# Token sums made by accumulating transfers instead of VectorE operations, in a hybrid convolution and attention layer

## The chip, the cores and the metric

The kernel runs on one core of one Trainium2 chip. The metric is the time of one execution in device microseconds (us); a kernel's time is the median of several executions. Engines are written as the profile has them: PE is TensorE's matmul, PEld its weight load, DVE is VectorE, ACT is ScalarE, POOL is GpSimd and SP is SyncE. PSUM is the memory that matmuls write, SBUF the memory on the chip, DRAM the one outside.

## The reference, cut to what matters

One layer of a model with two groups of tokens, 128 context tokens and 512 sample tokens, 1024 channels each. All 640 tokens go through one input projection `w_in` of 10240 columns; a long convolution (by a Fourier transform) and a neighbourhood attention work on parts of it, and the results are gated, projected and merged.

```python
def layer_forward(x, cond, ctx_kv, p):
    shift, scale, gate = modulation(cond, p["w_ada"], p["b_ada"])
    h = x * (1 + scale) + shift
    (v_h, x1, x0, g_h), (q, k, v, g_a), m = split_projection(h, p["w_in"], p["conv_w"], p["conv_b"])
    h_fwd, h_bwd = hyena_filters(...)
    y_h = hyena_long_conv(v_h, x1, x0, h_fwd, h_bwd, p["hyena_d"])
    ...
    out = merge_branches(y_h, g_h, y_a.reshape(g_a.shape), g_a, m, p["w_bh"], p["w_ba"], p["w_out"])
    x_new = layer_norm(ALPHA * x + gate * out, p["ln_g"], p["ln_b"])

def split_projection(h, w_in, conv_w, conv_b):
    z = h @ w_in
    ...

def hyena_long_conv(v_h, x1, x0, h_fwd, h_bwd, d_bias):
    u = v_h * x1
    ...
    y = jnp.fft.irfft(uf * ff[None], n=n, axis=1)[:, :L].astype(u.dtype)
    return (y + u * d_bias) * x0
```

The token sums of this case are no part of that formula. They come from a way of multiplying 2 by 2 blocks of `h` and `w_in` with seven products instead of eight, in which four of the left factors are sums and differences of blocks of `h`.

## The kernel before, in words

Every f32 operand of a matmul is kept as two halves, a high one of type F32R and a low one with the rest: `h` is `hH + hL` (tiles of 128 channels by 640 tokens, eight of them in each), a weight tile is `wh + wl`, and a product is three matmuls, hH by wh, hL by wh and hH by wl (`mm3`, L182). `split` (L99 to 102) makes such a pair: ScalarE copies the high half (L101) and VectorE subtracts it from the source (L102). For some weights (`eng="dma"`, L161 to 163) the low half is made without VectorE: ScalarE writes minus the high half into wl, GpSimd issues a transfer that adds the weights from DRAM to it (L162), and ScalarE copies the high half.

The run has these stages. A prologue makes `h` (to about 46 us). Three quarters follow, to about 300 us: `quarter_head`, `quarter_tail` and `values` make projection tiles of the convolution branch and the attention's values; woven into them are `long_conv`, `long_conv_back` and `filter_spectrum`, the Fourier transforms of the signal and the filter. Each projection tile ends in `conv_tile`: ScalarE copies two PSUM banks into one of two buffers `zs` (L481 to 485), scales it into the tile (L487), and VectorE adds the two neighbours (L489, two operations). A bank is free for the next tile but one when ScalarE has copied it, and `zs` when the second L489 has read it. The `fl` matmuls (L400, L401) start a class of the filter spectrum: VectorE makes `sd` of them (L406), ScalarE and VectorE split it into `sh` and `sl`, and TensorE takes those for `fa`, `fb`, `fc`, `fd` (L170 to 172). `yb` is the transform back, and L637 adds its result to u. After the quarters (about 300 us) come attention and the pair products with the seven-product scheme, whose matmuls are `sp<-t,wb` (L1235).

In that scheme the blocks of `h` are (i, j): i one of two halves of the channel tiles, j one of two halves of the tokens (`CS[j]`); r picks two of the channel tiles. For r = 0 and 1, `token_sums(r)` makes four sums, t1 = h00 - h01, t3 = h11 - h01, t2 = t1 + h11 and t4 = t2 - h10, each from high and low halves, in the tiles ts00, ts01 (for r = 0) and ts10, ts11. Before, VectorE made them: L714, L717, L718, L722, L723 and L703 (`step`), 128 by 640 each. `keep` splits each sum into high and low (the tiles t1.. to t4.., L101 and L102) and stores both in `tok_d` in DRAM by two transfers on GpSimd's queue (L712). Later `load_sums` reads them back; the first of these loads goes out at 304.7 us.

The order of the work comes from generators: `along` advances the token sums by one step after every sixth step of the quarter's main generator, and `weave` mixes main and convolution. Within the quarters a scheduler then chooses the order on each engine by its own estimates; only instructions marked with `keep_in_program_order` stay as written. Transfers of GpSimd are issued in the order of its queue, and a transfer that has to wait holds those behind it. The weight tiles are in rings: `raw` and `wh` two buffers, `wl` three.

Of the kernel before, what the change touches and what calls it, by code (L numbers as in the profile page):

```python
# [10 lines left out]
F32R = mybir.dt.float32r  # L11
AF = mybir.ActivationFunctionType
# [33 lines left out]
def tile_hyena_natten_step(ctx: ExitStack, tc: tile.TileContext, a, o):  # L46
    nc = tc.nc
    P = 128

    def f(ap):  # L50
        return ap.bitcast(F32)
# [4 lines left out]
    def two(t):  # L56
        return t.rearrange("p (a b) -> p a b", a=2)
# [10 lines left out]
    def weave(main, side, n_main, n_side):  # L68
        done, taken = 0, 0
        for _ in main:  # L70
            done += 1
            while taken * n_main < done * n_side:
                if next(side, StopIteration) is StopIteration:
                    break
                taken += 1
        for _ in side:
            pass
# [22 lines left out]
    def split(dst_h, dst_l, src, eng=None):  # L100
        hi = nc.scalar.activation(dst_h, src, AF.Copy)  # L101
        return hi, (eng or nc.vector).tensor_tensor(dst_l, src, f(dst_h), op=ALU.subtract)  # L102


    def row(pool, tag, name, dt=F32, bufs=NK + 1, n=NT):
        return pool.tile([P, NT + 4 if tag == "yh" else NT], dt, tag=tag, bufs=bufs, name=name)[:, :n]
# [395 lines left out]
    def quarter_head(q):  # L502
        us = []
        out[f"u{q}"] = us
        for i in range(2):
            n = 2 * q + i
            u = hw.tile([P, NG + 1], F32, tag="u", bufs=4, name=f"u{n}")
            x1 = hwa.tile([P, NG + 1], F32, tag="cv", bufs=2, name=f"x1_{n}")
            yield from conv_tile(n, u)
            yield  # L510
            yield from conv_tile(8 + n, x1)
            nc.vector.tensor_tensor(u[:, :NG], u[:, :NG], x1[:, :NG], op=ALU.mult)
            us.append(u)
            yield
# [10 lines left out]
    def quarter_tail(q):  # L525
        for i in range(2):
            n = 2 * q + i
            out["x0"][n] = row(yhp, "yh", f"x0_{n}", n=NG + 1)
            yield from conv_tile(16 + n, out["x0"][n])
            gate_conv(n)  # L530
            yield
# [111 lines left out]
    def values(m, home=None):  # L643
        w = [wtile(T_V + 2 * m + i, "dma", width=256) for i in range(2)]
        ps = [acc(f"v{m}_{i}") for i in range(2)]

        def passes(k):
            wh, wl = w[k // 4][0][k % 4], w[k // 4][1][k % 4]
            return ((hH, wh, k == 0, False), (hL, wh, False, False), (hH, wl, False, k == NK - 1))

        for half in range(2):
            ks = range(4 * half, 4 * half + 4)
            for k in ks:
                for x, wk, first, last in passes(k):
                    for t in range(4):
                        nc.tensor.matmul(  # L656
                            ps[t // 2][:, t % 2 * 256 : t % 2 * 256 + 256], x[:, k, P * t : P * t + P], wk,
                            start=first and t % 2 == 0, stop=last, skip_group_check=True,
                        )
                yield  # L660
            if half:
                parts = [ps[0][:], ps[1][:]]
            else:
                pe = acc(f"ve{m}")
            for k in ks:
                for x, wk, first, last in passes(k):
                    nc.tensor.matmul(pe[:, :256], x[:, k, P * 4 :], wk, start=first, stop=last, skip_group_check=True)  # L667
            yield
        if home is None:
            v = out[f"v{m}"] = slot(m, "v", f"v{m}")  # L670
            for c, p in ((0, parts[0]), (512, parts[1]), (1024, pe[:, :256])):
                nc.scalar.activation(v[:, c : c + p.shape[-1]], p, AF.Copy)
        else:
            for i, p in enumerate(parts):
                v = hwa.tile([P, NG + 1], F32, tag="cv", bufs=2, name=f"v{m}_{i}")
                nc.scalar.activation(v[:, :512], p, AF.Copy)
                nc.scalar.activation(v[:, 512:640], pe[:, 128 * i : 128 * i + 128], AF.Copy)
                nc.sync.dma_start(home[m][:, 512 * i : 512 * i + 512], v[:, :512])
                nc.sync.dma_start(home[m][:, 1024 + 128 * i : 1152 + 128 * i], v[:, 512:640])
                if i == 0:  # L680
                    nc.sync.dma_start(o["new_v"][:, m * 256 : m * 256 + 256], v[:, :256])
            yield
            return
        nc.sync.dma_start(o["new_v"][:, m * 256 : m * 256 + 256], v[:, :256])
        yield
# [11 lines left out]
    def token_sums(r):  # L697
        def part(t, i, j):
            return f(t[:, 4 * i + 2 * r : 4 * i + 2 * r + 2, CS[j]])

        def step(dst, i, j, op):
            for t in (hH, hL):
                nc.vector.tensor_tensor(dst, dst, part(t, i, j), op=op)  # L703

        a_, b_ = (two(row(yhp, "yh", f"ts{r}{i}")) for i in range(2))

        def keep(name, t):
            at_ = 4 * SUMS.index(name) + 2 * r
            hi, lo = (row(yhp, "yh", f"{name}{r}{i}", F32R) for i in range(2))
            split(two(hi), two(lo), t)  # L710
            for i, x in enumerate((hi, lo)):
                nc.gpsimd.dma_start(tok_d[at_ + i], f(x))  # L712

        ins = nc.vector.tensor_tensor(a_, part(hH, 0, 1), part(hL, 0, 1), op=ALU.add)  # L714
        tc.keep_in_program_order(ins)
        yield
        nc.vector.tensor_tensor(b_, part(hH, 0, 0), a_, op=ALU.subtract)  # L717
        nc.vector.tensor_tensor(b_, b_, part(hL, 0, 0), op=ALU.add)  # L718
        yield
        keep("t1", b_)  # L720
        yield
        nc.vector.tensor_tensor(a_, part(hH, 1, 1), a_, op=ALU.subtract)  # L722
        nc.vector.tensor_tensor(a_, a_, part(hL, 1, 1), op=ALU.add)  # L723
        yield
        keep("t3", a_)
        yield
        step(b_, 1, 1, ALU.add)
        yield
        keep("t2", b_)
        yield  # L730
        step(b_, 1, 0, ALU.subtract)
        yield
        keep("t4", b_)
        yield

    def braid(x, y):
# [8 lines left out]
    def chain(*gens):  # L745
        for g in gens:
            yield from g
# [11 lines left out]
    def along(main, side, every):  # L759
        for i, _ in enumerate(main):  # L760
            if i % every == 0:
                next(side, None)
            yield

    for q in range(3):
        weave(along(chain(quarter_head(q + 1), quarter_tail(q), values((2, 3, 1)[q], v_d)), sums, 6),
              chain(long_conv(q), braid(long_conv_back(q), filter_spectrum(q + 1))), 6 * NK + N_VALUES, N_CONV + N_BACK + N_FILTER)
    ident = out["ident"]

# [934 lines left out]
```

## Time and profile before

| what | us |
|---|---|
| median of 3 runs | 890.14 |
| lowest and highest | 889.31, 892.96 |
| the profiled execution | 889.48 |
| its span (first to last instruction) | 887.7 |
| busy: TensorE, VectorE, ScalarE, GpSimd | 869.3, 637.0, 450.6, 190.6 |
| token sums on VectorE, first and last | 67.6, 196.2 |
| token sums' stores issued, first and last | 72.3, 197.3 |

The profile shows one execution. A row of the timeline has its start, its length, the engine, the line, the operation with what it writes and reads (`out<-in`), and in brackets how long the engine had been idle and what ended that. A row of a group has its count behind an x, the busy time and the mean. A row of waits has the engine and line that waited, whom for, the total, the number and the longest. A row of transfers has the queue (SPq, POOLq), the count, the size of one and the median time from issue to landing.

### The profile page before, as it was taken

To read this page: it belongs to the slowest core of one execution; us is meant where nothing else is said; L and a number is where in the kernel's file an instruction comes from. 1 tells how busy PE (TensorE), PEld (TensorE's weight loads), DVE (VectorE), ACT (ScalarE), POOL (GpSimd) and SP (SyncE) were. 2 spreads that over 40 slices of the span, in tenths; PEclk is the share of its full clock that TensorE was granted. 3 is DMA by queue.
4 is the path that set the end of the run, shared out by engine and by line. 5 is a ranking of instruction groups with operands and counts; after the bars stand their busy time and mean duration, and the time that the engine had idled before them with its cause. 6 is when DMAs were issued, how large, how long until landed. Compare 5 with 4: busy or idle time off the path is not lost.

```text
span 887.7 us, 17134 instructions
## 1 busy us (share of the span) xinstructions
PE 869.3 (98%) x6476; PEld 837.6 (94%) x6476; DVE 637.0 (72%) x1215; ACT 450.6 (51%) x956; POOL 190.6 (21%) x216
## 2 busy tenths in 40 slices
PE   8999999899999999999999999999999999999996
PEld 6899999899899999899999999999999999999885
DVE  4779592996688459488877777777877666766666
ACT  4396454754554544467656566666566632243200
POOL 0012010221101021129354334333554200000000
PEclk9999999999999999999999999999999999999999
DMA  8978576678546697798686758675854576545521
GB/s 323 399 168 232 117 176 128 179 208 188 135 99 161 149 221 153 230 339 262 158 252 149 226 146 245 155 198 168 235 125 127 193 283 239 174 162 188 186 86 56
DMA packets 75247, 169.09 MB, mean 190 GB/s; under 512 B 11004, under 2 KB 28668, under 8 KB 75165
## 3 DMA queue, kind: packets, MB, share of 16 engines
q1 hardware_dynamic: 56204, 123.06, 41.4%
q0 software_dynamic: 13632, 39.33, 23.3%
q10 hardware_dynamic: 5328, 5.61, 1.8%
q8 instruction: 51, 0.84, 0.4%
q14 instruction: 32, 0.25, 0.1%
HBM read 143.32 MB, written 23.99 MB: 188 GB/s over the span
## 4 chain that ended last, share of the span: by engine, by line
PE 93%; DVE 4%; ACT 1%; DMA 1%; issue 0%; POOL 0%; SPq 0%; POOLq 0%; DVEq 0%; ACTq 0%
PE mm L182 34%; PE sp L1235 29%; PE out L1514 6%; PE v L656 5%; PE s L1041 2%; PE s L948 2%; PE pt L1032 2%; PE ve L667 1%; PE adaT L252 1%; DMA t<-tok_d 1%; DVE x L489 1%; PE yb L171 1%; PE adaT L269 1%; PE yb L172 1%; PE yb L170 0%
## 5 line engine op out<-in xcount | busy, mean ns | idle before, releaser
L1235 PE MATMUL sp<-t,wb 128*128 128x320 f32 x1008 | 159.0, 311 | 0.2 <-DMA t<-tok_d 0.2
L1235 PEld LDWEIGHTS sp<-t,wb 128*128 128x128 f32 x1008 | 150.0, 188 | 1.0 <-issue 0.5
L1235 PE MATMUL sp<-hH,wb 128*128 128x320 f32 x500 | 121.1, 313 | 0.0
L182 PE MATMUL mm<-hH,wh 128*128 128x320 f32 x336 | 83.9, 315 | 5.4 <-ACT zs L484 4.2
L1235 PEld LDWEIGHTS sp<-hH,wb 128*128 128x128 f32 x500 | 86.1, 188 | 2.6 <-issue 2.6
L162 POOL DMA_DIRECT2D wl<-wall x34 | 30.5, 897 | 255.6 <-ACT wl L161 239.0
L182 PE MATMUL mm<-hH,wl 128*128 128x320 f32 x336 | 82.4, 311 | 0.4 <-DVE wl L102 0.4
L182 PE MATMUL mm<-hL,wh 128*128 128x320 f32 x336 | 81.9, 310 | 0.0
L1235 PE MATMUL sp<-hL,wb 128*128 128x320 f32 x250 | 77.2, 309 | 0.0
L182 PEld LDWEIGHTS mm<-hH,wh 128*128 128x128 f32 x336 | 57.4, 188 | 8.0 <-ACT zs L484 5.1
L163 ACT ACTIVATE wh<-raw 128x1024 fp32r<-128x1024 f32 x34 | 36.1, 1062 | 56.7 <-PE mm L182 41.5
L1196 DVE TENSOR_TENSOR wb<-s,wb 128x512 fp32r<-128x512 f32 x63 | 45.3, 721 | 18.9 <-ACT wb L1188 18.7
L182 PEld LDWEIGHTS mm<-hH,wl 128*128 128x128 f32 x336 | 57.5, 188 | 1.2 <-DVE wl L102 0.9
L182 PEld LDWEIGHTS mm<-hL,wh 128*128 128x128 f32 x336 | 57.3, 188 | 0.6 <-DVE hL L329 0.5
L1003 POOL TENSOR_SCALAR p<-p,sm 128x384 f32<-128x384 f32 x32 | 52.0, 1721 | 22.7 <-PE sp L1235 9.3
L1003 POOL TENSOR_SCALAR edge<-edge,sm 128x320 f32<-128x320 f32 x32 | 42.9, 1500 | 62.1 <-DVE sm L1001 62.1
L1188 ACT ACTIVATE wb<-s 128x512 fp32r<-128x512 f32 x63 | 39.7, 631 | 31.1 <-PE sp L1235 19.3
L1235 PEld LDWEIGHTS sp<-hL,wb 128*128 128x128 f32 x250 | 47.0, 188 | 0.0
L1514 PE MATMUL out<-woh,yhs 128*128 128x512 f32 (+1 forms) x176 | 45.7, 373 | 0.0
L1223 DVE TENSOR_TENSOR spare_hHp<-sp,yu 128x320 f32<-128x320 f32 x63 | 30.5, 484 | 17.7 <-PE sp L1235 10.7
L182 PE MATMUL mm<-yhs,wh 128*128 128x320 f32 x224 | 42.0, 309 | 0.0
L1514 PEld LDWEIGHTS out<-woh,yhs 128*128 128x128 f32 x176 | 32.0, 188 | 6.4
(415 smaller groups left out, 2253.3 us busy)
## 6 DMA issues: line engine op xcount, KB each, us to landing
raw<-wall SPq DMA_DIRECT2D x54, 512.0 KB, 3.8
wl<-wall POOLq DMA_DIRECT2D x34, 512.0 KB, 6.7
ra<-wall SPq DMA_DIRECT2D x21, 512.0 KB, 5.0
rb<-wall SPq DMA_DIRECT2D x40, 256.0 KB, 5.4
ada<-wada SPq DMA_DIRECT2D x16, 512.0 KB, 8.0
tm<-bias SPq DMA_DIRECT2D x16, 512.0 KB, 7.5
s<-wall SPq DMA_DIRECT2D x21, 256.0 KB, 5.2
s<-wall POOLq DMA_DIRECT2D x21, 256.0 KB, 4.6
```

The source lines that it names most:

```text
L162: nc.gpsimd.dma_start(wl, a["wall"][i], accum_op=ALU.add)
L163: nc.scalar.activation(wh, raw[:], AF.Copy)
L182: nc.tensor.matmul(ps[hf][:, :HALF], wt[k], x[:, hf * HALF : (hf + 1) * HALF], start=(i == 0 and k == 0), stop=(i == lead[2] and k == NK - ...
L656: nc.tensor.matmul(ps[t // 2][:, t % 2 * 256 : t % 2 * 256 + 256], x[:, k, P * t : P * t + P], wk, start=first and t % 2 == 0, stop=last, ...
L948: nc.tensor.matmul(dst[h], x[rows(h), qs], y[rows(h), ks], start=i == 0, stop=i == 2, skip_group_check=True)
L1003: nc.gpsimd.tensor_scalar_mul(pv, pv, sm[:, 2, c : c + 1])
L1032: nc.tensor.transpose(pt[:, i * P : i * P + P], ps[h][:, c : c + P], ident)
L1188: nc.scalar.activation(made[g][:, 0], block(g), AF.Copy)
L1196: nc.vector.tensor_tensor(made[g][:, 1], block(g), f(made[g][:, 0]), op=ALU.subtract)
L1223: nc.vector.tensor_tensor(c, dst, c if j == 3 else ps["u"], op=ALU.add)
L1235: nc.tensor.matmul(dst, wk, x(xi, k), start=j < 4 and k == 0 and i == 0, stop=k == 3 and i == 2, skip_group_check=True,)
L1514: ins = nc.tensor.matmul(dst, m[k][:, c0 : c0 + P], w[:, c : c + n], start=(first and k == 0), stop=(last and k == 5), skip_group_check=True,)
```

## The change

`token_sums` no longer uses VectorE. Each sum is formed in its tile by transfers on GpSimd's queue: a plain copy of a block of hH, then accumulating ones (`accum_op=ALU.add`) for hL and the further blocks. A difference needs a turned sign: ScalarE multiplies the tile by -1 in place (`turned`). For the halves, ScalarE writes minus the sum into the low tile and the high half into the high tile (`halves`), and a transfer adds the sum to the low tile (`rest`); then both are stored as before. For each r that is 3 copies, 13 accumulating transfers and the same 8 stores, and on ScalarE 2 turns and 4 times 2 activations where 4 copies were. All these transfers are marked to stay in program order. A group has 16 steps, where there were 9, and `along` advances them after every fifth step of main instead of every sixth.

```diff
@@ -698,39 +698,71 @@
         def part(t, i, j):
             return f(t[:, 4 * i + 2 * r : 4 * i + 2 * r + 2, CS[j]])
 
-        def step(dst, i, j, op):
-            for t in (hH, hL):
-                nc.vector.tensor_tensor(dst, dst, part(t, i, j), op=op)
-
-        a_, b_ = (two(row(yhp, "yh", f"ts{r}{i}")) for i in range(2))
-
-        def keep(name, t):
-            at_ = 4 * SUMS.index(name) + 2 * r
-            hi, lo = (row(yhp, "yh", f"{name}{r}{i}", F32R) for i in range(2))
-            split(two(hi), two(lo), t)
-            for i, x in enumerate((hi, lo)):
-                nc.gpsimd.dma_start(tok_d[at_ + i], f(x))
-
-        ins = nc.vector.tensor_tensor(a_, part(hH, 0, 1), part(hL, 0, 1), op=ALU.add)
-        tc.keep_in_program_order(ins)
-        yield
-        nc.vector.tensor_tensor(b_, part(hH, 0, 0), a_, op=ALU.subtract)
-        nc.vector.tensor_tensor(b_, b_, part(hL, 0, 0), op=ALU.add)
-        yield
-        keep("t1", b_)
-        yield
-        nc.vector.tensor_tensor(a_, part(hH, 1, 1), a_, op=ALU.subtract)
-        nc.vector.tensor_tensor(a_, a_, part(hL, 1, 1), op=ALU.add)
-        yield
-        keep("t3", a_)
-        yield
-        step(b_, 1, 1, ALU.add)
-        yield
-        keep("t2", b_)
-        yield
-        step(b_, 1, 0, ALU.subtract)
-        yield
-        keep("t4", b_)
+        def queued(dst, src, **how):
+            tc.keep_in_program_order(nc.gpsimd.dma_start(dst, src, **how))
+
+        def add(dst, src):
+            queued(two(dst), src, accum_op=ALU.add)
+
+        def turned(t):
+            nc.scalar.activation(t, t, AF.Copy, scale=-1.0)
+
+        a_, b_ = (row(yhp, "yh", f"ts{r}{i}") for i in range(2))
+        kept = {}
+
+        def halves(name, t):
+            hi, lo = kept[name] = [row(yhp, "yh", f"{name}{r}{i}", F32R) for i in range(2)]
+            nc.scalar.activation(lo, t, AF.Copy, scale=-1.0)
+            nc.scalar.activation(hi, t, AF.Copy)
+
+        def rest(name, t):
+            add(f(kept[name][1]), two(t))
+            store(name, 0)
+
+        def store(name, i):
+            queued(tok_d[4 * SUMS.index(name) + 2 * r + i], f(kept[name][i]))
+
+        queued(two(b_), part(hH, 0, 0))
+        queued(two(a_), part(hH, 0, 1))
+        yield
+        add(b_, part(hL, 0, 0))
+        add(a_, part(hL, 0, 1))
+        yield
+        turned(a_)
+        yield
+        add(b_, two(a_))
+        yield
+        halves("t1", b_)
+        add(a_, part(hH, 1, 1))
+        yield
+        rest("t1", b_)
+        add(a_, part(hL, 1, 1))
+        yield
+        store("t1", 1)
+        add(b_, part(hH, 1, 1))
+        yield
+        halves("t3", a_)
+        add(b_, part(hL, 1, 1))
+        yield
+        rest("t3", a_)
+        yield
+        store("t3", 1)
+        queued(two(a_), part(hH, 1, 0))
+        yield
+        halves("t2", b_)
+        add(a_, part(hL, 1, 0))
+        yield
+        rest("t2", b_)
+        turned(a_)
+        yield
+        store("t2", 1)
+        add(b_, two(a_))
+        yield
+        halves("t4", b_)
+        yield
+        rest("t4", b_)
+        yield
+        store("t4", 1)
         yield
 
     def braid(x, y):
@@ -763,7 +795,7 @@
             yield
 
     for q in range(3):
-        weave(along(chain(quarter_head(q + 1), quarter_tail(q), values((2, 3, 1)[q], v_d)), sums, 6),
+        weave(along(chain(quarter_head(q + 1), quarter_tail(q), values((2, 3, 1)[q], v_d)), sums, 5),
               chain(long_conv(q), braid(long_conv_back(q), filter_spectrum(q + 1))), 6 * NK + N_VALUES, N_CONV + N_BACK + N_FILTER)
     ident = out["ident"]
```

In the changed kernel the transfers have L702, the turn L708, the halves L715 and L716; lines below `token_sums` are 32 higher.

What GpSimd's queue holds at the first group, from the first weight tile of the quarters on. The names: `wl2`, `wl10`, `wl3`, `wl11` are low halves of weight tiles, `ts00` and `ts01` the sums under way, `t100` and `t101` the high and low half of t1. Before:

```order
L162 DMA wl2_894<-wall 128x1024
L162 DMA wl10_1046<-wall 128x1024
L162 DMA wl3_1127<-wall 128x1024
L162 DMA wl11_1235<-wall 128x1024
L712 DMA tok_d_81<-t100_1087 128x640
L712 DMA tok_d_81<-t101_1088 128x640
```

The changed kernel there:

```order
L162 DMA wl2_894<-wall 128x1024
L702 DMA ts01_907<-hH_85 128x2x320
L702 DMA ts00_906<-hH_85 128x2x320
L702 DMA ts01_907<-hL_87 128x2x320
L162 DMA wl10_1047<-wall 128x1024
L702 DMA ts00_906<-hL_87 128x2x320
L162 DMA wl3_1124<-wall 128x1024
L702 DMA ts01_907<-ts00_906 128x640
L162 DMA wl11_1235<-wall 128x1024
L702 DMA ts00_906<-hH_85 128x2x320
L702 DMA t101_1192<-ts01_907 128x640
L702 DMA tok_d_81<-t100_1191 128x640
```

Seven transfers of the sums have moved in between and behind the weight tiles, each accumulating one behind the transfer whose result it needs; the add of hL into ts00 stands behind wl10, and wl3 and wl11 stand behind adds.

ScalarE at the halves of t3 in the first group. `zs` is the copy of a PSUM bank, `x1_2` a convolution tile, `sh0_1`, `sh0_3` and `sh0_4` are high halves for the filter spectrum, `raw16`, `wh16` and `wl16` a weight tile, `t300` and `t301` the halves of t3, `t200` the high half of t2. Before:

```order
L161 ACTIVATE wl16_1332<-raw16_1329 128x1024
L101 ACTIVATE sh0_1_781<-sd0_1_779 128x512
L101 ACTIVATE t300_1247<-ts00_906 128x640
L487 ACTIVATE x1_2_890<-zs1_109,pack2_380 128x641
L101 ACTIVATE t200_1403<-ts01_907 128x640
L101 ACTIVATE sh0_3_818<-sd0_3_816 128x512
L163 ACTIVATE wh16_1331<-raw16_1329 128x1024
L481 ACTIVATE zs0_105<-mm3_0_1131 128x128
```

The changed kernel there:

```order
L485 ACTIVATE zs1_109<-mm10_1_1052 128x8x40
L161 ACTIVATE wl16_1329<-raw16_1326 128x1024
L715 ACTIVATE t301_1384<-ts00_906 128x640
L716 ACTIVATE t300_1383<-ts00_906 128x640
L487 ACTIVATE x1_2_890<-zs1_109,pack2_380 128x641
L101 ACTIVATE sh0_3_818<-sd0_3_816 128x512
L101 ACTIVATE sh0_4_853<-sd0_4_851 128x512
L163 ACTIVATE wh16_1328<-raw16_1326 128x1024
L481 ACTIVATE zs0_105<-mm3_0_1128 128x128
```

Two activations of t3 stand ahead of `x1_2` and `sh0_3`, and wait for the transfer that completes ts00; the copy of t2 has left this place.

VectorE between the two L489 of the tile `x0_1`, towards the end of the first quarter. `sd1_3` and `sl1_3` belong to the filter spectrum, `u0` and `u1` are the convolution's signal (L628, L637), `yu0` and `yu1` its product with the gate x0, `t401` is the low half of t4. Before:

```order
L102 TENSOR_TENSOR sl1_3_1526<-sd1_3_1523,sh1_3_1525 128x512
L489 SCALAR_TENSOR_TENSOR x0_1_1470<-zs1_109,pack2_380,x0_1_1470 128x641
L637 SCALAR_TENSOR_TENSOR u0_676<-u0_676,hyd0_713,y0_1546 128x4x128
L637 SCALAR_TENSOR_TENSOR u1_733<-u1_733,hyd0_713,y1_1634 128x4x128
L102 TENSOR_TENSOR t401_1617<-ts01_907,t400_1616 128x640
L489 SCALAR_TENSOR_TENSOR x0_1_1470<-zs1_109,pack2_380,x0_1_1470 128x641
```

The changed kernel there:

```order
L102 TENSOR_TENSOR sl1_3_1522<-sd1_3_1519,sh1_3_1521 128x512
L489 SCALAR_TENSOR_TENSOR x0_1_1466<-zs1_109,pack2_380,x0_1_1466 128x641 x2
L637 SCALAR_TENSOR_TENSOR u0_676<-u0_676,hyd0_713,y0_1544 128x4x128
L471 TENSOR_TENSOR yu1_1632<-x0_1_1466,u1_733 128x128
L637 SCALAR_TENSOR_TENSOR u1_733<-u1_733,hyd0_713,y1_1626 128x4x128
```

The two L489 have come together, the L637 pair stands behind them, and t401 is gone. On TensorE the `fl1_3` matmul, which `sd1_3` reads, stands 88 rows ahead of the next tile's first matmul (mm13), where it stood 39 rows ahead; in the second quarter `fl2_3` stands 83 rows ahead of mm15's, where it stood 38; and the first `fc` of `sh0_3` stands at row 566 of TensorE, where it stood at 583.

## The prediction

> **What bounds the kernel now.** I read the page first: the busy shares, then the chain that ended last.
>
> ```profile
> span 887.7 us, 17134 instructions
> PE 869.3 (98%) x6476; PEld 837.6 (94%) x6476; DVE 637.0 (72%) x1215; ACT 450.6 (51%) x956; POOL 190.6 (21%) x216
> PE 93%; DVE 4%; ACT 1%; DMA 1%; issue 0%; POOL 0%; SPq 0%; POOLq 0%; DVEq 0%; ACTq 0%
> ```
>
> TensorE is busy for 98% of the span, and 93% of the last chain is its own work. The change leaves its work alone, so all it can save is TensorE's idle time in the stretch in which the sums are made and used. Next I read the table of windows from 60 to 400 us (columns: window, its length, PE, PEld, DVE, ACT, POOL busy, PE clock, DMA share, GB/s). Besides the first two rows, these are the windows in which TensorE is not busy all the time; in the others it shows 20.00 of 20.
>
> ```profile
> 60.00:80.00 20.00, 20.00 (x138) 19.82 (x138) 18.41 (x25) 14.22 (x29) 4.30 (x7) 1.00 0.82 205
> 80.00:100.00 20.00, 20.00 (x145) 19.81 (x143) 15.37 (x25) 10.49 (x21) 3.00 (x5) 1.00 0.77 197
> 140.00:160.00 20.00, 18.86 (x136) 18.22 (x134) 8.18 (x14) 8.61 (x12) 2.31 (x4) 1.00 0.54 114
> 160.00:180.00 20.00, 18.13 (x125) 17.64 (x126) 20.00 (x34) 13.03 (x30) 4.42 (x8) 1.00 0.69 188
> 220.00:240.00 20.00, 18.19 (x130) 17.46 (x129) 9.29 (x16) 9.47 (x16) 2.14 (x3) 1.00 0.53 113
> 240.00:260.00 20.00, 19.36 (x141) 19.09 (x140) 15.62 (x28) 12.00 (x29) 1.62 (x3) 1.00 0.45 107
> 340.00:360.00 20.00, 19.36 (x131) 18.34 (x129) 15.04 (x23) 10.19 (x19) 1.72 (x2) 1.00 0.56 113
> 360.00:400.00 40.00, 38.95 (x272) 37.49 (x273) 27.47 (x69) 20.99 (x55) 8.32 (x13) 1.00 0.99 319
> ```
>
> The idle time is 1.14 + 1.87 + 1.81 + 0.64 + 0.64 + 1.05 = 7.15 us, the ceiling of any gain here. VectorE is full around 60 and 160 us, where token sums stand, yet TensorE waits for nothing around 60. What it does wait for is in the list of TensorE's waits, from 130 to 182 us and then from 182 to 300:
>
> ```profile
> PE mm L182 <- ACT zs L484: 2.5, 1, 2.5
> PE c_X L171 <- DVE ul L102: 0.5, 1, 0.5
> ...
> PE mm L182 <- ACT zs L484: 1.8, 1, 1.8
> PE ut L540 <- ACT F L451: 0.6, 1, 0.6
> ```
>
> Together 5.4 us. The timeline shows how the first arises, and the second has the same form, of which its last row shows the end:
>
> ```profile
> 153.83 0.69 DVE L406 TENSOR_TENSOR sd<-fl,dec 128x512 f32<-128x512 f32 x1 [6.80 <-PE fl L401]
> 156.10 0.89 DVE L489 SCALAR_TENSOR_TENSOR x<-zs,pack,x 128x641 f32<-128x641 f32 x1
> 156.90 2.20 DVE L637 SCALAR_TENSOR_TENSOR u<-u,hyd,y 128x512 f32<-128x512 f32 x2
> 159.03 0.80 DVE L102 TENSOR_TENSOR t<-ts,t 128x640 fp32r<-128x640 f32 x1
> 159.76 0.87 DVE L489 SCALAR_TENSOR_TENSOR x<-zs,pack,x 128x641 f32<-128x641 f32 x1
> 160.72 0.28 ACT L481 ACTIVATE zs<-mm 128x128 f32<-128x128 f32 x1 [2.13 <-DVE x L489]
> 238.10 0.28 ACT L481 ACTIVATE zs<-mm 128x128 f32<-128x128 f32 x1 [2.05 <-DVE x L489]
> ```
>
> TensorE waits for a PSUM bank that ScalarE copies into zs; ScalarE waits until VectorE's second L489 has read the old zs; VectorE came to that late, because it had idled 6.80 us for fl (placed late on TensorE) and because two L637 and one `t` of the sums stood between its two L489.
>
> **The change, VectorE's side.** Eighteen `ts` operations and eight `t` go:
>
> ```profile
> L101 ACT ACTIVATE t<-ts x8: 722/748/812, 71.3 to 192.3; 128x640 fp32r<-128x640 f32 x8
> L102 DVE TENSOR_TENSOR t<-ts,t x8: 804/816/824, 74.0 to 196.2; 128x640 fp32r<-128x640 f32 x8
> L714 DVE TENSOR_TENSOR ts<-hH,hL x1: 820/820/820, 67.6 to 67.6; 128x640 f32<-128x640 f32 x1
> ```
>
> These are the copies that ScalarE makes of the sums, the eight `t` of VectorE, and the first of the eighteen: 26 x 0.815 = 21.2 us of VectorE, nearly all beside TensorE's work. What they are worth is the waits above. In the changed order the two L489 before the first wait follow each other with no L637 or `t` between (the L637 pair and the `t` are 2.20 + 0.80 = 3.0 us, more than the 2.5 of the wait), and fl stands 88 rows of TensorE ahead of the waiting matmul instead of 39. At 20 us for 136 matmuls that is 49 x 0.147 = 7.2 us earlier. The 1.8 has the same form, with 83 rows instead of 38. I take both as gone, and with them the 0.5 and 0.6, which depend on the same late VectorE: **-5.4 us**. Between 0 (they come back elsewhere) and -7.15, this is the end that the rows explain.
>
> **The transfers.** On GpSimd's queue 32 transfers join the 16 stores: 26 accumulating ones and 6 copies, 327,680 bytes each. No row shows a 320 KB accumulate. The nearest, by issue to landing (the windows 60 to 80, 80 to 100 and 150 to 180, then the page, then the tile `t`):
>
> ```profile
> wl<-wall POOLq DMA_DIRECT2D x3, 512.0 KB, 7.1
> tok_d<-t POOLq DMA_DIRECT2D x4, 320.0 KB, 5.4
> ...
> tok_d<-t POOLq DMA_DIRECT2D x3, 320.0 KB, 6.6
> ...
> tok_d<-t POOLq DMA_DIRECT2D x6, 320.0 KB, 3.1
> ...
> raw<-wall SPq DMA_DIRECT2D x54, 512.0 KB, 3.8
> wl<-wall POOLq DMA_DIRECT2D x34, 512.0 KB, 6.7
> s<-wall SPq DMA_DIRECT2D x21, 256.0 KB, 5.2
> s<-wall POOLq DMA_DIRECT2D x21, 256.0 KB, 4.6
> q0 software_dynamic: 13632, 39.33, 23.3%
> ...
> DMA to landing us min/median/max: 2.5/5.1/6.8
> ```
>
> `wl` and the POOLq `s` accumulate already. The first sums stand where the DMA share is 0.82 and 0.77, so a link lands between 5.4 and 7.1 us; I take L = 6.0, midway between the two stores of the same size there. Wherever it is quiet, 3 to 4.6 is nearer.
>
> These links are in series, and ScalarE now waits inside its own order for three of them (turned, the t1 halves, the t3 halves). With these rows the first group can be laid out:
>
> ```profile
> 49.23 1.02 POOL L162 DMA_DIRECT2D wl<-wall  x1 [47.70 <-ACT wl L161]
> 56.59 0.87 POOL L162 DMA_DIRECT2D wl<-wall  x1 [6.34 <-ACT wl L161]
> 62.51 0.93 ACT L487 ACTIVATE x<-zs,pack 128x641 f32<-128x641 f32 x1
> 81.69 0.63 ACT L101 ACTIVATE sh<-sd 128x512 fp32r<-128x512 f32 x1 [2.35 <-DVE sd L406]
> 85.95 0.27 PE L170 MATMUL fc<-sh,dftH 128*128 128x256 f32 x1
> ```
>
> The first copies go out behind the `wl` of 49.23; the add of hL into ts00 stands behind the `wl` of 56.59, so it goes at 57.5 and lands at 57.5 + L. ScalarE turns it (0.75, as a `t<-ts`; ScalarE comes there at 62.5). Three links follow, each waiting for the last: ts01 += ts00, ts00 += hH, ts00 += hL. The t3 halves can start at 57.5 + L + 0.85 + 3L = 58.35 + 4L: 78.4 for L = 5, 82.4 for 6, 86.8 for 7.1. Behind them on ScalarE stand the L487 of x1 and `sh` for TensorE's `fc`. The `fc` of 85.95 stands 17 rows earlier in the changed order, 17 x 0.145 (20 us for 138 matmuls) = 2.5 us, so `sh` must end by 83.4. Less 0.63 for itself, 0.93 for L487 and 2 x 0.75 for the halves, the sum must have landed by 80.3. Cost = 58.35 + 4L - 80.3: 0 up to L = 5.5, **2.1 us at 6.0**, 4.4 at 6.6, 6.4 at 7.1. The `wl` that now queue behind blocked links are covered by three buffers; the one at 56.59 keeps its place.
>
> The other groups (from about 130 us on) run where windows show shares of 0.45 to 0.69 and most links land before ScalarE comes: 0 to 2, I take **0.5**. ScalarE's own extra (8 lows and 4 turns, 12 x 0.75 = 9 us) lies in an engine busy 8.6 to 14.2 of 20: nothing. The 10.5 MB added need, at queue q0's rate (39.33 MB in 23.3% of 887.7 us, 190 GB/s), 55 us of all 16 engines. That is why L is not taken at its quiet value.
>
> Against this change speaks a rule of the Trainium skill: "Collectives: The Full Stack", section on the bandwidth ceiling, says that an adding transfer needs two source reads and moves at about half the rate of a copy. The pair raw 3.8 and wl 6.7 agrees, the pair `s` 5.2 and 4.6 does not. By it a link would be nearer 5.4 x 1.76 = 9.5 us (an estimate), and the first group alone would cost 16: the stretched case below, driven further.
>
> **Sum.** The profiled execution took 889.48 (887.7 and 1.8 outside): 889.48 - 5.4 + 2.1 + 0.5 = 886.7. The median shown, 890.14, lies 0.66 above, so the forecast is 887.3. About 0.5% (4.45 us) is what a measurement of this kernel can tell from no change: faster means below 885.7, slower above 894.6.
>
> **Rivals.** *All hidden.* Links land in 5.5 us or less even at the start, the groups cost nothing: 884.1, by the median 884.7, with the ceiling 882.9. For: lone stores land in 2.5 to 3.1. Against: 5.4 and 6.6 in the very windows. In the Trainium skill, "DMA: Bandwidth & Descriptors", the section on one SWDGE transfer fits 2.0 us plus bytes over 436 GB/s, 2.75 us here (an estimate), which leads to this case; only the minimum of 2.5 in the trace agrees, the median of 5.1 does not.
>
> *The links stretch.* The copies, adds and stores of the first group saturate a queue already at 0.8, and a link takes 8 us. `wl` in that window shows 7.1 without this load. The t3 halves then wait until 90.35, `sh` and TensorE with them: 10 us, and 1 elsewhere: 889.48 - 5.4 + 10 + 1 = 895.1, by the median 895.8. It decides above L = 7.8; up to 6.6 it is repaid.
>
> *The waits come back.* The scheduler has moved matmuls earlier everywhere, and the new place meets its producers as late as the old one: the gain is 0 to 2 and the cost stays, 890 to 893. For: VectorE is at 20.00 of 20 in the window 160 to 180, which shows how little freedom its neighbours have. Against: the wait's cause (the L637 pair and `t` between two L489) is gone from the order.
>
> **Chances.** Forecast (L from 5.5 to 6.6, the waits gone; 885 to 889.6) 0.40, all hidden 0.24, waits back 0.18, stretched 0.18. Faster: all hidden and 0.06 of the forecast's lower end, 0.30. Slower: stretched and 0.04 of waits back with some stretch, 0.22. Same: the rest, 0.48. For 8 in 10 the range takes the hidden case down to its ceiling, 883, and the stretched one up to L = 8.2 (11 + 1), 897.
>
> **What would show it.** In the changed profile: no `mm <- ACT zs` wait near 160 and 237 us (if they are there, the gain's step is wrong); ts and t transfers on POOLq landing in 5.5 to 6.6 us at 50 to 90 us (this decides between hidden, forecast and stretched); ScalarE waiting for `ts` by about 2 us at each of three places before 90, TensorE for `fc <- sh` by 2. A wait of TensorE for `wl`, or for W's halves at `yb`, would be a cost that I set at nothing.

## The result and the profile after

The changed kernel takes 916.33 us (median of 4 runs, 914.93 to 918.93), the kernel before 890.88 beside it (4 runs): ratio 1.029, interval 1.025 to 1.032. The change makes the kernel slower by some 25 us, where 887.3 was forecast.

The page of the profile after, its span, the busy shares and the chain that ended last:

```profile
span 912.9 us, 17166 instructions
...
PE 879.2 (96%) x6476; PEld 846.8 (93%) x6476; DVE 620.0 (68%) x1189; ACT 459.1 (50%) x968; POOL 221.9 (24%) x248
...
PE 75%; issue 10%; DMA 8%; DVE 3%; ACT 2%; POOL 2%; POOLq 0%; ACTq 0%; DVEq 0%
```

Two things are seen. TensorE's own part of the chain has fallen from 93% to 75%; transfers now hold 8% of it and "issue" 10%. These shares are not a loss by themselves: 48.2 us of "issue" are GpSimd's idle time from 1.5 to 49.7 us, which stands in the chain because the chain now leads back through its queue. And TensorE's busy time has grown, 869.3 to 879.2, with the same 6476 matmuls. So the 25.2 us of span are 9.9 us of slower matmuls and 15.3 us more idle (33.7 for 18.4).

The table of windows, those of 20 us (the last of 40) between 60 and 400 us in which TensorE idles (columns as in the prediction):

```profile
60.00:80.00 20.00, 16.94 (x103) 16.13 (x102) 9.95 (x14) 10.79 (x24) 8.11 (x9) 0.91 0.92 179
80.00:100.00 20.00, 17.54 (x113) 16.93 (x112) 11.31 (x20) 10.86 (x22) 7.50 (x8) 0.91 1.04 227
...
180.00:200.00 20.00, 17.84 (x122) 17.00 (x121) 11.19 (x18) 11.02 (x23) 7.14 (x8) 1.00 1.02 243
200.00:220.00 20.00, 16.79 (x135) 16.52 (x134) 17.07 (x22) 11.40 (x20) 6.54 (x7) 0.97 0.91 202
...
260.00:280.00 20.00, 16.15 (x114) 15.62 (x112) 5.66 (x9) 9.72 (x19) 5.95 (x8) 1.00 0.97 218
280.00:300.00 20.00, 18.63 (x129) 18.36 (x130) 15.93 (x18) 8.34 (x15) 3.68 (x5) 0.83 0.62 152
...
360.00:400.00 40.00, 35.37 (x226) 34.01 (x226) 27.32 (x43) 15.07 (x27) 5.03 (x10) 0.91 0.62 168
```

The idle time is 20.7 us, where it was 7.1, in three places at which sums are made (5.5 us from 60 to 100, 5.4 from 180 to 220, 5.2 from 260 to 300) and behind the last quarter (4.6 from 360 on). The clock column falls to 0.91 and 0.83 in windows with gaps. The DMA share in the first window rose from 0.82 to 0.92, in the second from 0.77 to 1.04.

The waits of TensorE over the whole run, those above 1 us in 60 to 400:

```profile
PE c_X L170 <- ACT uh L101: 3.8, 2, 2.1
PE mm L182 <- DMA wl<-wall: 3.7, 2, 3.2
PE p_X L170 <- ACT uh L101: 3.2, 1, 3.2
PE fb L170 <- ACT sh L101: 2.6, 1, 2.6
PE yb L170 <- ACT ph L101: 2.5, 1, 2.5
PE fc L170 <- ACT sh L101: 2.5, 1, 2.5
PE yb L171 <- DVE pl L102: 1.2, 1, 1.2
```

The four waits that the prediction took away (`mm <- ACT zs` twice, `c_X <- DVE ul`, `ut <- ACT F`) are gone. In their place TensorE waits for operands that ScalarE makes (`sh`, `uh`, `ph`) and for `wl`. Why ScalarE is late is in its own waits (40 to 320 us) for the turns L708 and the halves L715:

```profile
ACT t L715 <- DMA ts<-ts: 13.5, 3, 5.1
...
ACT t L715 <- DMA ts<-hL: 10.9, 2, 6.2
ACT ts L708 <- DMA ts<-hL: 7.6, 2, 7.3
...
ACT ts L708 <- DMA ts<-hLp: 4.1, 1, 4.1
```

That is 36.1 us in eight waits, where before it waited for no transfer of the sums. The first group in the timeline, GpSimd's issues, ScalarE's two long waits and TensorE's answer to the second:

```profile
50.49 1.77 POOL L702 DMA_DIRECT2D ts<-hH  x2
59.40 1.21 POOL L702 DMA_DIRECT2D ts<-hL  x1 [7.13 <-DMA ts<-hH]
60.13 1.43 POOL L162 DMA_DIRECT2D wl<-wall  x1
60.74 2.05 POOL L702 DMA_DIRECT2D ts<-hL  x1
...
70.31 0.74 ACT L708 ACTIVATE ts<-ts 128x640 f32<-128x640 f32 x1 [7.32 <-DMA ts<-hL]
...
75.61 1.19 POOL L702 DMA_DIRECT2D ts<-hH  x1 [0.70 <-DMA ts<-ts]
...
83.86 1.20 POOL L702 DMA_DIRECT2D ts<-hL  x1 [5.56 <-issue]
89.00 0.74 ACT L715 ACTIVATE t<-ts 128x640 fp32r<-128x640 f32 x1 [6.22 <-DMA ts<-hL]
...
91.75 0.38 PE L170 MATMUL fc<-sh,dftH 128*128 128x256 f32 x1 [2.46 <-ACT sh L101]
```

The first add went out 8.9 us behind the copies that it needs (50.49 to 59.40; the copies land after 8.6), and the add that stands between two `wl` took 9.5 us (60.74 to 70.31). The t3 halves start at 89.0. And the transfers' times over the run:

```profile
tok_d<-t POOLq DMA_DIRECT2D x16, 320.0 KB, 5.6
...
ts<-hH POOLq DMA_DIRECT2D x8, 320.0 KB, 7.5
ts<-hL POOLq DMA_DIRECT2D x8, 320.0 KB, 6.3
t<-ts POOLq DMA_DIRECT2D x8, 320.0 KB, 6.6
...
ts<-ts POOLq DMA_DIRECT2D x4, 320.0 KB, 5.5
...
ts<-hHp POOLq DMA_DIRECT2D x2, 320.0 KB, 9.5
```

The rows of accumulating links have medians of 5.5 to 6.6 us. The plain copies are not below them: both of `ts<-hHp` (9.5) and four of the eight `ts<-hH` are copies, the other four are adds.

The slower matmuls are seen in windows of 4 us at the gaps (columns as above; the clock is the third from the end):

```profile
88.00:92.00 4.00, 1.54 (x11) 1.27 (x10) 0.79 (x1) 2.69 (x4) 0.18 (x1) 1.00 1.13 234
92.00:96.00 4.00, 4.00 (x21) 3.82 (x21) 4.00 (x8) 2.67 (x7) 1.19 (x1) 0.59 0.95 172
...
280.00:284.00 4.00, 2.63 (x10) 2.44 (x11) 2.92 (x5) 1.35 (x4) 1.43 (x3) 0.55 0.77 180
284.00:288.00 4.00, 4.00 (x23) 4.00 (x23) 2.86 (x6) 3.69 (x8) 1.36 (x2) 0.59 0.63 209
```

After the gap of 2.46 us that ends at 91.75, TensorE does 21 matmuls in 4 us where it does 29 to 32 at full clock in the windows around. At the gap of 3.17 that ends at 281.37 the lower clock lasts for some 7 us.

### The profile page after: what moved, and what is told of

The parts are those of the page before. It is cut to its first block, busy times and chain, and to the rows that moved or that the text cites. A ratio compares the mean times of both kernels' runs of the same rounds, so it can differ in the third digit from the quotient of the medians.

```text
span 912.9 us, 17166 instructions
## 1 busy us (share of the span) xinstructions
PE 879.2 (96%) x6476; PEld 846.8 (93%) x6476; DVE 620.0 (68%) x1189; ACT 459.1 (50%) x968; POOL 221.9 (24%) x248
## 4 chain that ended last, share of the span: by engine, by line
PE 75%; issue 10%; DMA 8%; DVE 3%; ACT 2%; POOL 2%; POOLq 0%; ACTq 0%; DVEq 0%
PE sp L1267 29%; PE mm L182 22%; PE out L1546 6%; PE v L656 4%; DMA ts<-hL 2%; PE s L1073 2%; PE s L980 2%; PE pt L1064 2%; DMA ts<-ts 1%; DMA ts<-hH 1%; DMA wl<-wall 1%; PE ve L667 1%; DMA ts<-hLp 1%; DMA t<-ts 1%; POOL ts L702 1%
## 5 line engine op out<-in xcount | busy, mean ns | idle before, releaser
L182 PE MATMUL mm<-hH,wh 128*128 128x320 f32 x336 | 81.4, 315 | 1.2 <-ACT hH L328 0.6
L162 POOL DMA_DIRECT2D wl<-wall x34 | 32.8, 969 | 196.6 <-ACT wl L161 164.6
L182 PEld LDWEIGHTS mm<-hH,wh 128*128 128x128 f32 x336 | 57.5, 191 | 2.7 <-ACT hH L328 0.8
L1035 POOL TENSOR_SCALAR p<-p,sm 128x384 f32<-128x384 f32 x32 | 50.1, 1646 | 23.7 <-PE sp L1267 9.8
L489 DVE SCALAR_TENSOR_TENSOR x<-zs,pack,x 128x641 f32<-128x641 f32 x32 | 28.3, 883 | 35.0 <-ACT x L487 34.4
```

The lines of the kernel that those rows point to most:

```text
L162: nc.gpsimd.dma_start(wl, a["wall"][i], accum_op=ALU.add)
L182: nc.tensor.matmul(ps[hf][:, :HALF], wt[k], x[:, hf * HALF : (hf + 1) * HALF], start=(i == 0 and k == 0), stop=(i == lead[2] and k == NK - ...
L489: nc.vector.scalar_tensor_tensor(d, zs[:, c : c + NG], convw[:, i, c : c + 1], d, op0=ALU.mult, op1=ALU.add)
L1035: nc.gpsimd.tensor_scalar_mul(pv, pv, sm[:, 2, c : c + 1])
```

## The experiments

The theories: A, ScalarE in its order waits for links of 6 to 9.5 us and holds TensorE's operands behind them; B, the added traffic and the longer GpSimd queue cost by themselves; C, the scheduler's new order costs by itself. All ratios are to the kernel before, timed beside the variant.

**One half alone: low halves by transfer** (lows_only), sums on VectorE:

```diff
-            split(two(hi), two(lo), t)
-            for i, x in enumerate((hi, lo)):
-                nc.gpsimd.dma_start(tok_d[at_ + i], f(x))
+            nc.scalar.activation(two(lo), t, AF.Copy, scale=-1.0)
+            nc.scalar.activation(two(hi), t, AF.Copy)
+            nc.gpsimd.dma_start(f(two(lo)), t, accum_op=ALU.add)
+            nc.gpsimd.dma_start(tok_d[at_], f(hi))
+            kept.append((tok_d[at_ + 1], f(lo)))
```

The last store goes out at the next step of the generator.

> Half of the change alone: the sums stay on VectorE, only their low halves are made by ScalarE (minus the sum, and the high half) and one accumulating transfer, with the store of the low half one step later. ScalarE waits for no transfer here. Theory A (links of 6 to 9.5 us, for which ScalarE waits in its order): 885 to 890, no gap of TensorE of 2 us or more that before did not have. Theory B (the added traffic and the blocked GpSimd queue cost by themselves): a quarter of the transfers, 893 to 897. Theory C (a new order by the scheduler costs by itself): cannot be told in advance, anything from 885 to 897, with the loss after the last values matmul.

893.73 us, ratio 1.001 (1.000 to 1.003): no change that can be measured. The time lies outside A's range and inside B's and C's, and TensorE has a new gap of over 2 us, which A did not allow. Two rows suggest why A's gain stayed out, one of TensorE's waits and one of VectorE's timeline:

```profile
PE fz L390 <- issue: 3.7, 1, 3.7
```

```profile
186.72 0.82 DVE L703 TENSOR_TENSOR ts<-ts,hH 128x640 f32<-128x640 f32 x1 [7.61 <-DMA t<-ts]
```

VectorE wants to form t2 over t1, which a transfer still reads, and stands for 7.61 us; TensorE's gap of 3.7 us, which the profile puts down to "issue", ends 3.0 us behind that start. That the one led to the other is tried in the last experiment (lows_own_tile).

**The other half alone: sums by transfers** (sums_only), low halves by `split` on VectorE:

```diff
-            nc.scalar.activation(lo, t, AF.Copy, scale=-1.0)
-            nc.scalar.activation(hi, t, AF.Copy)
+            split(hi, lo, t)
 
         def rest(name, t):
-            add(f(kept[name][1]), two(t))
             store(name, 0)
```

> The other half alone: the sums are made by transfers and ScalarE's turn as in the changed kernel, the low halves by VectorE as before. ScalarE still waits for the sums at the same six places per group. Theory A: 908 to 918, with ScalarE's waits for transfers near 60 to 70 and 82 to 89 us still there. Theory B: three quarters of the transfers, 907 to 912. Theory C: the loss after the last values matmul decides, 905 to 916.

907.7 us, ratio 1.018 (1.014 to 1.022): in B's and C's ranges and 0.3 us below A's, so it decides nothing between them. ScalarE still waits 30.4 us for transfers of the sums, as A has it. The run shows that most of the loss comes with the sums. TensorE's two longest waits in 60 to 400 us:

```profile
PE fc L170 <- ACT sh L101: 3.5, 1, 3.5
PE fa L170 <- ACT sh L101: 2.9, 1, 2.9
```

**ScalarE without the waits** (act_free), all transfers in place:

```diff
-            nc.scalar.activation(t, t, AF.Copy, scale=-1.0)
+            nc.scalar.activation(two(spare_), part(hH, 0, 1), AF.Copy, scale=-1.0)
...
-            nc.scalar.activation(lo, t, AF.Copy, scale=-1.0)
-            nc.scalar.activation(hi, t, AF.Copy)
+            nc.scalar.activation(two(lo), part(hH, 0, 1), AF.Copy, scale=-1.0)
+            nc.scalar.activation(two(hi), part(hH, 0, 1), AF.Copy)
```

> The changed kernel with all its 48 transfers in the same chain on GpSimd's queue, but ScalarE's turns and halves read a block of hH, which is ready, instead of the sums (so the sums are not computed rightly: signs and high halves are left out). ScalarE waits for no transfer of the sums. Theory A: 887 to 896, the gaps of TensorE for sh, uh and ph gone, at most 3 to 4 us left for a late wl. Theory B: 908 to 916, since traffic and queue are as in the changed kernel. Theory C: 896 to 902, the 6 us after the last values matmul stay.

894.77 us, ratio 1.004 (1.002 to 1.006): 21.6 us below the changed kernel, with the same 48 transfers in the same chain. This is in A's range and below both B's and C's. TensorE's busy time is 869.4 again, so the slower matmuls have gone together with ScalarE's waits. What stays are waits for `wl`, the list of TensorE's waits in 60 to 400:

```profile
PE mm L182 <- DMA wl<-wall: 4.6, 2, 3.4
PE v L656 <- DMA wl<-wall: 1.9, 4, 0.9
```

These 6.5 us are B's part.

**More room for each transfer** (paced), two empty steps of the generator ahead of each step of ScalarE (one ahead of the second turn), and a step after every third of main:

```diff
+        yield
+        yield
         turned(a_)
...
+        yield
+        yield
         yield
         halves("t1", b_)
...
-        weave(along(chain(...), sums, 5),
+        weave(along(chain(...), sums, 3),
```

> The changed kernel with the same work, but every step on ScalarE put two generator steps further behind its transfer (27 steps, one after every third step of main, instead of 16 after every fifth). Theory A: the transfers get about 13 us of main's work where they had 7, so ScalarE's waits fall under 1 us each and the time to 890 to 902. Theory B: as the changed kernel, 912 to 918. Theory C: 900 to 916 with gaps of TensorE that name no transfer.

914.87 us, ratio 1.025 (1.021 to 1.029): none of A's gain, a time in B's and C's ranges. But the room was not given: ScalarE's waits for the sums are 41.4 us, where A asked for under 1 us each. The timeline of ScalarE shows the turn and the t1 halves where they were in the changed kernel (70.31 and 75.40 there):

```profile
69.80 0.74 ACT L708 ACTIVATE ts<-ts 128x640 f32<-128x640 f32 x1 [6.74 <-DMA ts<-hL]
...
74.88 0.76 ACT L715 ACTIVATE t<-ts 128x640 fp32r<-128x640 f32 x1
```

The transfers are marked to stay in program order, ScalarE's steps are not; those go where the scheduler puts them. So the run says nothing against A, and it gave a second question: is it the scheduler that puts them too early (A2), or is the chain too long wherever they are put (A1)?

**ScalarE's steps kept in program order** (act_pinned), and the same on the spaced variant (paced_pinned); for the turn and both halves:

```diff
-            nc.scalar.activation(lo, t, AF.Copy, scale=-1.0)
+            tc.keep_in_program_order(nc.scalar.activation(lo, t, AF.Copy, scale=-1.0))
```

> The changed kernel, only that the turns and halves on ScalarE are also kept in program order, so that the scheduler cannot put them ahead of what main has issued before. Theory A2 (the scheduler takes the transfers as landed sooner than they are and puts ScalarE's steps too early, which is why the spaced variant changed nothing): the steps move back to about 7 us behind their transfers, ScalarE's waits fall from 36 us to 10 to 20, time 898 to 908. Theory A1 (the place is not the scheduler's doing, the chain is simply too long for where main needs it): 912 to 918 as the changed kernel.

898.84 us, ratio 1.009 (1.008 to 1.011): 17.5 us of the loss gone by pinning alone, within A2's range. Half of what the span gained (912.9 to 896.9) is TensorE's busy time, 879.2 to 871.2. ScalarE's waits (40 to 320 us) have fallen from 36.1 to 23.6 us, not quite to the 10 to 20 that A2 expected:

```profile
ACT ts L708 <- DMA ts<-hL: 10.5, 3, 7.3
...
ACT t L715 <- DMA ts<-hL: 6.7, 1, 6.7
...
ACT t L715 <- DMA ts<-ts: 6.4, 2, 4.9
```

> The spaced variant (two generator steps more between a transfer and ScalarE's use of it) with ScalarE's steps kept in program order. Theory A2: about 13 us of main's work lie between, more than a link's 6 to 9 us, so ScalarE waits for almost nothing and the time is that of the variant in which ScalarE waits for no transfer, 891 to 898. Theory A1: 908 to 918.

903.36 us, ratio 1.014 (1.012 to 1.016): better than the changed kernel, but outside the ranges of both A2 and A1, and slower than without the spacing. ScalarE waits 32.4 us for the sums, where A2 expected almost nothing. One wait of ScalarE is 9.72 us long (timeline):

```profile
198.56 0.74 ACT L708 ACTIVATE ts<-ts 128x640 f32<-128x640 f32 x1 [9.72 <-DMA ts<-hLp]
```

GpSimd issued that add at 188.87, 0.6 us behind a `wl`. That link took 9.7 us. So the place on ScalarE is a large part, and even with it a link can be longer than the room that it got; why the spacing made things worse was not tried.

**Links of few bytes** (tiny_links), every accumulating transfer cut to 32 columns:

```diff
-            queued(two(dst), src, accum_op=ALU.add)
+            queued(two(dst)[:, :1, :32], src[:, :1, :32], accum_op=ALU.add)
```

> The changed kernel with every accumulating transfer cut to 32 of its 640 columns (the sums then lack most of their terms), copies and stores as they are, the same chain and the same waits of ScalarE. If a link is long because of its bytes and of the traffic around it, links land in 2 to 4 us, ScalarE's waits fall by half or more and the time comes to 890 to 902. If a link is long by itself (a fixed time, the queue's order), links still land in 5 to 7 us and the time stays at 908 to 918.

889.1 us, ratio 0.998 (0.997 to 1.000), just below the first expectation's range and far from the second's. The links shorten. The rows of three kinds of link (in the changed kernel 6.3, 6.6 and 5.5), and the row of all transfers of the tile `ts`, the uncut copies among them (min, median, max; in the changed kernel 3.7, 6.7, 9.9):

```profile
ts<-hL POOLq DMA_DIRECT2D x8, 16.0 KB, 4.7
t<-ts POOLq DMA_DIRECT2D x8, 16.0 KB, 3.1
...
ts<-ts POOLq DMA_DIRECT2D x4, 16.0 KB, 3.7
```

```profile
DMA to landing us min/median/max: 2.0/4.2/8.9
```

With a twentieth of the bytes a link still takes half to three quarters of its time, so a large part of it does not come from its own bytes. What went with the bytes, the link's own and those that other links meet, is 1.6 to 3.5 us a link; the run does not part the two. It was enough to bring ScalarE's waits from 36.1 to 14.1 us and to take the whole loss away.

**Both taken away** (act_free_tiny), the two edits above together:

> Both costs taken away at once: ScalarE's turns and halves read a block of hH instead of the sums, and every accumulating transfer carries 32 of 640 columns (so the sums are left out in two ways; copies and stores stay). What is left is VectorE's relief and the new order. If the relief is worth the 5.4 us that the prediction gave it: 883 to 887. If the relief is worth nothing and the spaces are filled by other waits: 888 to 891. With the three runs before it this splits the loss into ScalarE's waits and the bytes.

884.73 us, ratio 0.993 (0.990 to 0.995). The four kernels form a square:

| us | ScalarE waits | ScalarE doesn't wait |
|---|---|---|
| full links | 916.3 | 894.8 |
| tiny links | 889.1 | 884.7 |

VectorE's relief, together with the new order, is worth some 6 to 7 us (890.9 to 891.8 for the kernel before, beside these four). The bytes cost 10 us by themselves, ScalarE's waits 4 by themselves, and both together 31.6: most of the loss needs long links and a ScalarE that waits for them.

**Low halves where nothing is overwritten** (lows_t3_t4): the kernel before, with lows_only's edit for t3 and t4, and `split` for t1 and t2.

> The kernel before with only the low halves of t3 and t4 made by ScalarE and an accumulating transfer: no later operation of VectorE overwrites those two sums, so VectorE cannot be held by the transfer that still reads a sum, as it was for 7.6 us in the variant with all four low halves. ScalarE waits for no transfer. If that hold was what cost the variant its gain: 884 to 889, with no gap of TensorE of 2 us near 190. If the relief of VectorE is worth nothing: 889 to 893.

887.18 us, ratio 0.996 (0.995 to 0.998): 0.4% below the kernel before, within the expected range, and no gap near 190.

**A tile of its own for t2** (lows_own_tile): lows_only, and

```diff
-        def step(dst, i, j, op):
-            for t in (hH, hL):
-                nc.vector.tensor_tensor(dst, dst, part(t, i, j), op=op)
+        def step(dst, src, i, j, op):
+            nc.vector.tensor_tensor(dst, src, part(hH, i, j), op=op)
+            nc.vector.tensor_tensor(dst, dst, part(hL, i, j), op=op)
...
-        step(b_, 1, 1, ALU.add)
+        step(c_, b_, 1, 1, ALU.add)
...
-        step(b_, 1, 0, ALU.subtract)
+        step(b_, c_, 1, 0, ALU.subtract)
```

> All four low halves by ScalarE and a transfer, the sums on VectorE, but t2 is formed in a tile of its own instead of over t1, so that VectorE's next sum does not overwrite what a transfer still reads. If the 7.6 us hold of VectorE near 180 cost the variant with four low halves its gain: 884 to 889, at least as fast as the variant with t3 and t4 alone, and no gap of 3.7 us near 190. If the gap had another cause: 891 to 895 as before.

884.73 us, ratio 0.993 (0.990 to 0.995), as fast as the square's last cell. The hold of VectorE and the gap of 3.7 are gone; the largest waits of TensorE in 46 to 410 us are

```profile
PE mm L182 <- ACT zs L484: 1.1, 2, 0.7
PE c_X L171 <- DVE ul L102: 0.9, 1, 0.9
```

So eight operations taken from VectorE (8 x 0.816 = 6.5 us of its time) gave as much as the change wanted from 26. What the tile of its own does with the low halves left to VectorE was not tried.

## Why the prediction was wrong, step by step

**VectorE's relief, -5.4 us: the waits named are gone, the size agrees in part by luck.** The four waits are absent from the changed profile, and with the two costs taken away (act_free_tiny) the kernel lies 0.73% (6.5 us) below the one before. But only part of that is the idle time that the prediction counted: TensorE's idle time from 60 to 400 us falls from 7.15 to 4.2 us there, a new wait of 2.6 for `wl` included. Its busy time, which the prediction held to be untouched, falls too, 869.3 to 867.2, and no run tells why.

**The first group's chain: L = 6.0 a little small, its start misplaced.** The sum for t3 was there at 89.0, where the formula gives 82.4. Of the 6.6 us between, 3.2 are the start. The prediction hid the copies behind one `wl` and let the next, that of 56.59, keep its place; in the order of the changed queue that one (wl10) stands behind both copies and behind an add that has to wait for a copy. It went out at 60.13, and the add of hL into ts00 at 60.74 instead of 57.5. The four links in series then took 9.5, 4.0, 7.7 and 5.1 us, 6.6 on average, the upper end of the forecast: 2.3 us more than four times 6.0. The last 1 us lies between landings and the issues behind them. The prediction bounded L by stores and `wl` in a profile without this load, added up that the load would be 55 us of all engines, and still took the middle of those rows. Even so L as an average was not what failed; a single L hides the add of 9.5 us, for which ScalarE waited 7.32.

**The first group, 2.1 us: too small, its mechanism right.** Lateness of ScalarE passed to TensorE where the prediction said (`fc <- ACT sh`, 2.46 us), and one place earlier too (`fb <- ACT sh`, 2.58, behind the turn that waited 7.32). The idle time of the first two windows is 5.5 us. The formula, fed with 89.0, would have asked for 8.7; TensorE was itself later by then, through the earlier gap and the slower matmuls behind it.

**The other groups, 0.5 us: this is the step that failed most.** Their idle time is 5.4 and 5.2 us, and 4.6 behind the last quarter. The prediction took shares of 0.45 to 0.69 from before as the quiet in which links land in time. Those were the windows in which TensorE idled, not those in which the links would run: the links ran from 166 to 216 and from 244 to 284 us, and the windows from 160 to 220 and from 240 to 280 stand at 0.86 to 1.02 with the change. And it took it that ScalarE comes late enough; the scheduler had put its steps too early for these links, and keeping them in program order gave 17.5 us back. The 4.6 us of the last windows (`yb <- ACT ph`) were not taken apart: in act_free TensorE idles 1.6 us in all of 300 to 400, but no run isolates them.

**The clock: a term that the sum put at nothing.** 9.9 us are matmuls at a lower granted clock. It was 1.00 in every window of before, with gaps of 2.5 and 1.8 us, so the prediction priced a gap at its length. In the changed kernel the clock reads 0.50 around the end of five gaps of 2.46 to 3.21 us, for 3.4 us at three of them and 6.8 at two. That the loss of clock comes from the gaps was read from their order in the traces, not tried by itself; it fits that act_free, which has one gap of over 2 us left and lost no clock there, has TensorE's busy time of before.

**`wl`, priced at nothing: 3.7 us** in the changed kernel, 6.5 in act_free. Three buffers did not cover it.

**The rivals.** "The links stretch" had the mechanism and the sign; it gave 895.8, since it put 1 us on the later groups and nothing on the clock. "All hidden" gave 884.7, and the square's last cell shows that very figure, but with both costs taken away and partly by other terms; that is luck. "The waits come back" is refuted for the changed kernel: they did not. The range ended at 897 because it moved only L in the first group and left the terms at 0.5 and at nothing where they were.

**The rule against the change.** The sentence from the Trainium skill, that an adding transfer moves at half the rate of a copy ("Collectives: The Full Stack", the bandwidth ceiling), gave 9.5 us a link and 16 for the first group. The page says it of the adding step of a collective. It came nearer than the forecast, but not by its reason: the pairs of copies here took 8.6 and 9.5 us, the rows of adds have medians of 5.5 to 6.6.

## What to carry to other kernels

In this case transfers paid in place of vector operations only where no compute engine that feeds the bound engine has to wait for a link in its own order: here low halves by one transfer, read by nobody but a store, gained 0.7% once VectorE's next sum went to another tile than the one that the transfer reads, and the chain with six turns and halves per group lost 2.9%. Price a link at the load that the change itself makes, and look at what an engine's order was built on: the scheduler here put the readers of transfers too early, and pinning those readers gave back 17 of 25 us. Take the traffic that a transfer will meet from the windows in which it will run, not from those in which the bound engine idles. A gap of the bound engine costs more than its length if the clock falls after it.

## What the runs showed of the hardware

**A gap's price is not fixed.** Gaps of 2.46 us (after), 2.58 (after) and 3.21 (after) were followed by half the clock, and in lows_t3_t4 one of 1.78 (ending at 160.96); one of 2.48 (before, ending at 161.34) and one of 3.37 (act_free) were not. From 60 to 400 us each stretch of lower clock lasted 3.4 or 6.8 us, whatever the gap. The loss also changes between executions of one program: of 47 executions of the kernel before (those beside act_free, act_pinned and act_free_tiny), the 15 with a mean granted clock of 0.997 or more have a median of 889.4 us, the other 32 of 891.9. The windows around the gap of act_free, which ends at 69.59:

```profile
64.00:68.00 4.00, 2.22 (x16) 1.86 (x14) 1.50 (x3) 4.00 (x11) 0.42 (x1) 1.00 1.12 238
68.00:72.00 4.00, 2.41 (x16) 2.41 (x17) 3.75 (x5) 3.36 (x9) 1.31 (x2) 1.00 1.07 279
```

The Trainium skill, "TensorE: Matmul & The Clock Gate", part 1, tells of a window of about 3.4 us that runs freely and halves the clock after an idle one. The scatter agrees with a window whose phase the kernel doesn't set, and so do the stretches of 3.4 and 6.8 us. That 2.46 us were enough does not agree with a whole idle window, and the measurement decides.

**Copies within SBUF were no faster than accumulating transfers** of the same size on the same queue: the first pair of copies took 8.6 us and the second pair 9.5, against medians of 6.3 for the adds of hL and 5.5 for ts into ts. These copies go out in pairs beside a `wl`, which may be the reason; it was not tried. A copy that went out by itself, at 104.83, took 5.8.

**An accumulating link keeps much of its time without its bytes.** At 16 KB instead of 320 KB the rows of adds have medians of 2.8 to 4.7 us (tiny_links), against 5.5 to 6.6 in the changed kernel.
